# Strassen's seven products for four of eleven blocks of the up projection of a channel mixer

## The chip, the cores and the metric

One core of one Trainium2 chip runs the kernel. The metric is device time in microseconds (us) of one execution, lower is better; times are compared as medians over executions on the same chip. The engines of the core are named as the profile names them: PE is TensorE's matrix multiply, PEld its weight load, DVE is VectorE, ACT is ScalarE, POOL is GpSimd, SP is SyncE, which here only starts transfers.

## What is computed

The reference is a two-layer encoder on 512 tokens of 1024 channels. Each layer has a token mixer (layer 0: retention beside neighbourhood attention, layer 1: a Mamba-2 scan) and then the channel mixer that the change touches. Cut to that channel mixer:

```python
def conv_geglu_ffn(hn, w_up, conv_w, conv_b, w_down):
    u = depthwise_conv_centered(hn @ w_up, conv_w, conv_b)    # width 3 along the tokens
    gate, val = jnp.split(u, 2, axis=-1)                      # 2816 channels each
    return (jax.nn.gelu(gate, approximate=True) * val) @ w_down
...
    f = conv_geglu_ffn(rms_norm(x, norm_ffn_pre[layer]), ffn_w_up[layer], ...)
    x = x + rms_norm(f, norm_ffn_post[layer])
```

`w_up` is 1024 x 5632, `w_down` 2816 x 1024, all in float32. The change concerns the product `hn @ w_up`.

## The kernel before

**Precision.** A float32 product is made of three passes of TensorE in a 32-bit format of fewer mantissa bits (`R32`). Each operand is split into a high and a low part (`split`, L104: ScalarE casts the high part, L107; VectorE subtracts it from the original, L108), and `mm3` (L114) issues three matmuls into the same PSUM bank: high x high (L116), the stationary operand's low part x the other's high part (L117), and high x low (L118).

**Up projection.** `ffn` (L385) holds the normalised tokens feature-major, split already, in `E.xh` and `E.xl`: eight slices of 128 channels by 512 tokens. The 2816 gate and 2816 value channels are 22 tiles of 128 each. For a tile f, `wload` (L73) brings the gate weights, 128 x 1024 numbers, 512 KB, to a staging tile `wst`, `wunit` (L81) splits them to `whi` and `wlo`, and `proj_fm` (L127) runs 8 x 3 matmuls of 128 x 128 weights against 512 tokens into one PSUM bank; the value tile follows in the same way. I call such a load with its split and its 24 matmuls a unit. The first two tiles of a mixer are made in halves of 256 tokens, so that they can start before the last tokens are normalised. `tail` (L401) then makes the convolution out of PSUM (`conv`, L393: one step on ScalarE, L396, two on VectorE, L397 and L398), the GELU on ScalarE (L403) and the product gate x value on VectorE (L405) into `H`, 22 x 512 columns.

**Buffers.** There are 3 staging tiles, 4 each of `whi` and `wlo`, 2 of `gain` (a row of norm weights on all partitions), 7 of `tmp`, and eight PSUM banks, four in `mm` and four in `px` (L38 to L48). The up projection uses the four `mm` banks, two a tile.

**Down projection.** `down_strassen` (L278) already makes the down product by Strassen's method in Winograd's form. `sums` (L262) has the quarters of `w_down` added by accumulating transfers on GpSimd's queue (L274), into DRAM; these are cut into 32 `chores`, two of which are released after each tile, each waiting for the last matmul issued so far (`chore`, L68). The four quarters of `H` are combined by VectorE in `raw` (L308): the first difference (L311) goes into a tile `s3` of its own, the others into `H` in place. `prepare` (L322) splits them. The operand of the first of the seven products is split in `ffn`, L439 to L443, after tile 14 (`f == HK + 3`), into the buffers `b1h` and `b1l`. 

**Order.** The program is written in one stream. A scheduler places each instruction on its engine's queue by the order of the program and by when it reckons the operands and buffers ready; `high_priority(60)` moves a weight split ahead by 60 places. On the chip each queue then runs in that fixed order, with semaphores between the engines. All weight loads are on SyncE's queue.

Of the kernel before, what the change touches and what calls it, by code (L numbers as in the profile page):

```python
# [8 lines left out]
F32 = mybir.dt.float32  # L9
R32 = mybir.dt.float32r  # L10
# [3 lines left out]
ALU = mybir.AluOpType  # L14
# [3 lines left out]
P = 128  # L18
S = 512
NT = S // P  # L20
D = 1024
# [3 lines left out]
NF = FFN // P  # L25
HK = NF // 2
HW = S // 2
# [250 lines left out]
def down_strassen(E, big, pool, w, ts, H, s3, first, g_post, done):  # L278
# [7 lines left out]
    k0 = [0]  # L286

    def stage(i, u, cols):
        st = pool.tile([P, 1024], F32, name="wx") if k0[0] % 4 == 3 else E.wst.tile([P, 1024], F32, name="wst")
        k0[0] += 1  # L290
        nc.sync.dma_start(st[:, :cols], quarters(*i)[u])
        return st[:, :cols]
# [15 lines left out]
    def raw(i):  # L308
        tt, stt = nc.vector.tensor_tensor, nc.vector.scalar_tensor_tensor
        if i == 1:  # L310
            tt(s3, A11, A21, op=ALU.subtract)  # L311
            return s3
        if i == 2:
            tt(A21, A22, A21, op=ALU.subtract)
            stt(A11, A11, -1.0, A21, op0=ALU.mult, op1=ALU.subtract)
            return A11
        if i == 6:
            stt(A11, A12, -1.0, A11, op0=ALU.mult, op1=ALU.subtract)
            return A11
        return {3: A22, 4: A21, 5: A12}[i]  # L320
# [16 lines left out]
    for i, (src, bank) in enumerate(seq):  # L337
# [32 lines left out]
        op = nxt  # L370
        for t in range(2):
            if i in (0, 1, 2):
                kept[i, t] = pool.tile([P, 512], F32, name=f"k{i}{t}")
# [10 lines left out]

def ffn(E, w_up, cw, w_down, ts, g_post_row, done, w1=None):  # L385
# [3 lines left out]
    with ExitStack() as ctx:  # L389
# [3 lines left out]
        def conv(ps, s, f):  # L393
            w = lambda i: cwt[:, s, f, i:i + 1]
# [6 lines left out]
        def tail(f, pg, pv):  # L401
            g = conv(pg, 0, f)
            nc.scalar.activation(g, g, AF.Gelu_apprx_tanh)  # L403
            v = conv(pv, 1, f)
            nc.vector.tensor_tensor(H[:, f], g, v, op=ALU.mult)  # L405
# [11 lines left out]
        s3 = hp.tile([P, HK, HW], F32, name="s3")  # L417
        cwt = cp.tile([P, 2, NF, 4], F32, name="cwt")
        nc.sync.dma_start(cwt, cw)
        p0 = [[E.mm.tile([P, S], F32, name="mm") for s in range(2)] for f in range(2)]  # L420
# [6 lines left out]
        for f in range(2):  # L427
            tail(f, *p0[f])
        for f in range(2, NF):
            ps = []  # L430
# [8 lines left out]
            if f == HK + 3:  # L439
# [5 lines left out]
        down_strassen(E, hp, cp, w_down, ts, H, s3, first, g_post, done)  # L445
# [887 lines left out]
```

## Time and profile before

| what | value |
|---|---|
| timed runs, median of 3 | 1386.52 us (1384.4 to 1386.54) |
| profiled execution, its own time | 1384.75 us |
| its span | 1383.0 us |
| mean granted TensorE clock | 0.998 |
| HBM read, written | 221.01 MB, 51.64 MB |

The two channel mixers lie in the middle and at the end of the span: the one of layer 0 from about 272 to 640 us, the one of layer 1 from about 1031 to 1383 us. In each the up projection comes first, the down projection last; in layer 0 the down products start at 515.7 us, in layer 1 at 1270.9 us.

How to read what is shown of the profile: in a row of a group stand the line of the kernel, the engine, the operation, the output and inputs by the program's names, their shape and the count, then the busy time in us and the mean of one in ns, then the engine's idle time just before these instructions and what ended it. In the order of time, a line begins with the start and the length in us. In a table of windows, each engine has its busy time and, in brackets, its instructions; then come the granted clock, the busy share of the transfer engines and GB/s. Matmuls are pipelined: their records overlap, and the distance between starts tells how fast they go.

### The profile page before, as it was taken

How to read it: one execution, taken by the hardware profiler on the slowest of the kernel's cores; microseconds unless marked ns; L12 is line 12 of the kernel's file. 1: busy time of each engine (PE TensorE's matmuls, PEld its weight loads, DVE VectorE, ACT ScalarE, POOL GpSimd, SP SyncE). 2: the span in 40 equal slices, each digit the busy share in tenths (PEclk: the TensorE clock that was granted, in tenths of full speed). 3: DMA queues.
4: the chain of work that ended last, by engine and by line, in shares of the span. 5: the costliest groups of instructions: out<-in, count | busy, mean ns of one | idle time of the engine just before them, and what ended most of it. 6: DMA issues, size and time to landing. Idle time of an engine off the chain costs nothing.

```text
span 1383.0 us, 18079 instructions
## 1 busy us (share of the span) xinstructions
PE 1356.4 (98%) x6776; PEld 1119.3 (81%) x6776; DVE 985.0 (71%) x1402; ACT 758.2 (55%) x1233; POOL 113.6 (8%) x130
## 2 busy tenths in 40 slices
PE   7999999999999999999999999999999999999997
PEld 6877777898888888888778788787888888888886
DVE  7378888655565559697878785898786556556976
ACT  5357666443343346664878787487554434334563
POOL 0011110100011100020000110010010001110000
PEclk9999999999999999999999999999999999999999
DMA  8443222236679926553566464174445668983654
GB/s 295 145 141 105 90 87 95 69 143 230 233 204 233 236 88 187 197 202 127 144 180 191 125 186 158 54 208 119 138 133 172 217 228 223 226 220 96 200 177 144
DMA packets 69368, 229.81 MB, mean 166 GB/s; under 512 B 8352, under 2 KB 9120, under 8 KB 68768
## 3 DMA queue, kind: packets, MB, share of 16 engines
q1 hardware_dynamic: 54224, 167.30, 37.1%
q0 software_dynamic: 7168, 46.14, 13.6%
q10 hardware_dynamic: 7888, 15.21, 4.1%
q8 instruction: 54, 0.88, 0.3%
q14 instruction: 34, 0.28, 0.1%
HBM read 221.01 MB, written 51.64 MB: 197 GB/s over the span
## 4 chain that ended last, share of the span: by engine, by line
PE 85%; DVE 5%; ACT 4%; DMA 2%; issue 2%; POOL 1%; SPq 0%; DVEq 0%; POOLq 0%; ACTq 0%
PE mm L116 25%; PE mm L118 25%; PE mm L117 25%; DMA pb<-pd 2%; PE pi L999 1%; PE st L948 1%; PE py L1019 1%; ACT pb L978 1%; DVE wlo L108 1%; PE pt L173 1%; PE y L674 1%; DVE xs L164 1%; PE pt L892 1%; ACT whi L107 1%; DMA wst<-in_ab_v 0%
## 5 line engine op out<-in xcount | busy, mean ns | idle before, releaser
L116 PE MATMUL mm<-xh,whi 128*128 128x512 f32 (+1 forms) x1216 | 463.9, 382 | 1.0 <-ACT z L918 0.5
L118 PE MATMUL mm<-xl,whi 128*128 128x512 f32 (+2 forms) x1216 | 463.2, 381 | 1.0 <-DVE xl L108 0.5
L117 PE MATMUL mm<-xh,wlo 128*128 128x512 f32 (+2 forms) x1216 | 462.8, 381 | 1.0 <-DVE wlo L108 1.0
L108 DVE TENSOR_TENSOR wlo<-wst,whi 128x1024 fp32r<-128x1024 f32 (+1 forms) x232 | 281.0, 1215 | 72.7 <-ACT whi L107 72.1
L107 ACT CAST whi<-wst 128x1024 fp32r<-128x1024 f32 (+1 forms) x232 | 238.5, 1032 | 107.2 <-PE mm L117 63.5
L116 PEld LDWEIGHTS mm<-xh,whi 128*128 128x128 f32 x1216 | 228.3, 188 | 45.9 <-issue 2.5
L118 PEld LDWEIGHTS mm<-xl,whi 128*128 128x128 f32 (+1 forms) x1216 | 228.1, 188 | 45.5 <-issue 1.3
L117 PEld LDWEIGHTS mm<-xh,wlo 128*128 128x128 f32 (+1 forms) x1216 | 228.4, 188 | 44.2 <-DVE wlo L108 1.4
L397 DVE SCALAR_TENSOR_TENSOR cv<-mm,cwt,cv 128x511 f32<-128x511 f32 x88 | 65.9, 749 | 171.7 <-ACT cv L396 171.7
L396 ACT ACTIVATE cv<-mm,cwt 128x512 f32<-128x512 f32 x88 | 68.7, 780 | 200.4 <-PE mm L118 200.4
L978 ACT ACTIVATE pb<-pb,tok 128x128 f32<-128x128 f32 x256 | 80.9, 392 | 10.1 <-DMA pb<-pd 8.7
L398 DVE SCALAR_TENSOR_TENSOR cv<-mm,cwt,cv 128x511 f32<-128x511 f32 x88 | 66.0, 750 | 2.8
L116 PE MATMUL mm<-whi,ab1h 128*128 128x512 f32 x164 | 64.0, 390 | 0.0
L118 PE MATMUL mm<-wlo,ab1h 128*128 128x512 f32 x164 | 63.9, 390 | 0.0
L117 PE MATMUL mm<-whi,ab1l 128*128 128x512 f32 x164 | 63.8, 389 | 0.0
L403 ACT ACTIVATE cv<-cv 128x512 f32<-128x512 f32 x44 | 27.8, 633 | 44.5 <-DVE cv L398 44.4
L912 DVE SCALAR_TENSOR_TENSOR xf<-mm,cwt,xf 128x511 f32<-128x511 f32 (+1 forms) x64 | 47.6, 745 | 6.3 <-ACT xf L909 5.9
L274 POOL DMA_DIRECT2D ts<-in_f_down x48 | 30.0, 650 | 268.5 <-PE mm L118 266.0
L1031 POOL TENSOR_TENSOR sq<-sq 128x512 f32<-128x512 f32 x11 | 17.5, 1594 | 308.8 <-ACT sq L1025 245.1
L116 PE MATMUL mm<-whi,yh 128*128 128x512 f32 x104 | 40.8, 394 | 1.7 <-DVE xf L912 1.7
L117 PE MATMUL mm<-whi,yl 128*128 128x512 f32 x104 | 41.1, 395 | 0.0
L116 PE MATMUL mm<-whi,xh 128*128 128x512 f32 x104 | 40.7, 398 | 0.0
(308 smaller groups left out, 2121.6 us busy)
## 6 DMA issues: line engine op xcount, KB each, us to landing
wst<-in_f_up SPq DMA_DIRECT2D x88, 512.0 KB
ts<-in_f_down POOLq DMA_DIRECT2D x48, 704.0 KB, 5.8
wst<-in_c_fm SPq DMA_DIRECT2D x40, 512.0 KB
wst<-ts SPq DMA_DIRECT2D x32, 512.0 KB
pb<-pd ACTq DMA_DIRECT2D x29, 512.0 KB
wst<-in_f_down SPq DMA_DIRECT2D x24, 512.0 KB
ts<-ts POOLq DMA_DIRECT2D x16, 704.0 KB, 8.2
wst<-in_ab_fm SPq DMA_DIRECT2D x20, 512.0 KB
```

Of the source, the lines that this page charges most:

```text
L107: first = self.nc.scalar.copy(hi, src)
L108: second = self.nc.vector.tensor_tensor(lo, src, hi.bitcast(F32), op=ALU.subtract)
L116: mm(out, lh, rh, start=first, stop=False)
L117: mm(out, ll, rh, start=False, stop=False)
L118: self.product = mm(out, lh, rl, start=False, stop=last)
L274: out.append(lambda i=i, src=src, j=j, c=c, kw=kw: gp.dma_start(part(ts, i, c), part(src, j, c), **kw))
L396: nc.scalar.activation(o, ps, AF.Identity, scale=w(1), bias=w(3))
L397: nc.vector.scalar_tensor_tensor(o[:, 1:], ps[:, :S - 1], w(0), o[:, 1:], op0=ALU.mult, op1=ALU.add)
L398: nc.vector.scalar_tensor_tensor(o[:, :S - 1], ps[:, 1:], w(2), o[:, :S - 1], op0=ALU.mult, op1=ALU.add)
L403: nc.scalar.activation(g, g, AF.Gelu_apprx_tanh)
L912: nc.vector.scalar_tensor_tensor(r[:, a], ps[:, b], wc(j), r[:, a], op0=ALU.mult, op1=ALU.add)
L978: nc.scalar.activation(pb[:, dr, c], pb[:, dr, c], AF.Identity, scale=1.0 - 2 * dr, bias=tok[:, 0, c, dr * H + h:dr * H + h + 1])
```

## The change

In each mixer the tiles 6 and 7, 10 and 11, 14 and 15, and 18 and 19 become blocks of two gate and two value tiles. Such a block is one matrix product of 512 channels (256 gate, 256 value) by 1024 by 512 tokens; each side is halved, and `up_strassen` makes the quarters' product from seven products of 256 x 512 x 256 instead of eight. The other seven pairs of tiles stay as they were.

- *Token operands.* `combos` makes four sums and differences of the token quarters (`R1`, `S3`, `S2`, `S4`) on VectorE and splits them, one in each of tiles 2 to 5. It reads the quarters back as high + low into the part of `H` that tiles 14 to 21 will fill. The split results lie in the buffers `b1h`, `b1l`, `s3` and `e2` until the last block. Three operands are the split tokens themselves.
- *Weight operands.* Four loads of 512 KB bring the weight quarters, three to staging tiles and one to a `gain` tile. VectorE makes four sums of them in place; each of seven operands is split to `whi` and `wlo`, with the priority of the weight splits.
- *Products.* Each is 2 x 4 x 3 matmuls of 128 x 128 weights against 256 tokens. Product 1, 3, 5 and 7 go into the banks `a` (`mm`), 2 and 4 into `b`, 6 into `d` (both `px`); 3, 4, 5 and 7 add to what stands in their bank. After products 1, 2, 3, 5 and 7 ScalarE copies the two banks' state out to `G`, `V` or a temporary tile; after 4, 5 and 6 VectorE adds.
- *Tails.* The convolutions of a block read `G` and `V` in SBUF. `V` holds the negative, so that a table `cwn` with the sign turned is made once.
- *Moves.* The split of the first down operand comes after tile 20 instead of 14; the first difference of the down product takes the buffer `s3` that `S2` held; the kept results and a staging tile of the down projection share buffers with `G` and `V`. Chores: two after products 3 and 6 of a block.

The diff, without its blank lines:

```diff
--- before.py
+++ after.py
@@ -275,7 +275,7 @@
     return out
-def down_strassen(E, big, pool, w, ts, H, s3, first, g_post, done):
+def down_strassen(E, big, pool, w, ts, H, first, g_post, done):
@@ -286,7 +286,7 @@
     k0 = [0]
     def stage(i, u, cols):
-        st = pool.tile([P, 1024], F32, name="wx") if k0[0] % 4 == 3 else E.wst.tile([P, 1024], F32, name="wst")
+        st = pool.tile([P, 1024], F32, name="wx", tag="k3") if k0[0] % 4 == 3 else E.wst.tile([P, 1024], F32, name="wst")
         k0[0] += 1
         nc.sync.dma_start(st[:, :cols], quarters(*i)[u])
         return st[:, :cols]
@@ -308,6 +308,7 @@
     def raw(i):
         tt, stt = nc.vector.tensor_tensor, nc.vector.scalar_tensor_tensor
         if i == 1:
+            s3 = big.tile([P, HK, HW], F32, name="s3")
             tt(s3, A11, A21, op=ALU.subtract)
             return s3
         if i == 2:
@@ -368,9 +369,11 @@
             if uu == (1,):
                 nxt = prepare(i + 1)
         op = nxt
+        if i in (0, 1, 2):
+            m = pool.tile([P, 2, 512], F32, name="k", tag=f"k{i}")
+            kept.update({(i, t): m[:, t] for t in range(2)})
         for t in range(2):
             if i in (0, 1, 2):
-                kept[i, t] = pool.tile([P, 512], F32, name=f"k{i}{t}")
                 nc.scalar.copy(kept[i, t], bank[t])
             else:
                 j, tok, n = {3: (2, 0, 0), 4: (1, 0, 1), 5: (0, 2, 0)}[i]
@@ -382,6 +385,114 @@
     E.late += [lambda s=s: E.finish(s, st, done) for s in LATE]
+UP = (6, 10, 14, 18)
+def combos(E, pool, raw):
+    tt, stt = E.nc.vector.tensor_tensor, E.nc.vector.scalar_tensor_tensor
+    f32 = lambda ap: ap.bitcast(F32)
+    lower, upper = slice(0, HW), slice(HW, S)
+    out = {}
+    block = lambda k, c: (slice(None), slice(4 * k, 4 * k + 4), c)
+    def whole(i, k, c):
+        b = block(k, c)
+        tt(raw[:, i], f32(E.xh[b]), f32(E.xl[b]), op=ALU.add)
+        return raw[:, i]
+    def parts(n, tag, src):
+        x = pool.tile([P, 2, 4, HW], R32, name="x" + n, tag=tag)
+        E.split(x[:, 0], x[:, 1], src)
+        out[n] = x[:, 0], x[:, 1]
+    for n, k, c in (("A11", 0, upper), ("A12", 1, upper), ("A22", 1, lower)):
+        out[n] = E.xh[block(k, c)], E.xl[block(k, c)]
+    r1, a21 = whole(0, 1, lower), whole(1, 0, lower)
+    tt(r1, r1, a21, op=ALU.subtract)
+    parts("R1", "b1h", r1)
+    yield out
+    s2 = whole(2, 0, upper)
+    tt(a21, s2, a21, op=ALU.subtract)
+    parts("S3", "b1l", a21)
+    yield out
+    stt(s2, s2, -1.0, r1, op0=ALU.mult, op1=ALU.subtract)
+    parts("S2", "s3", s2)
+    yield out
+    s4 = whole(3, 1, upper)
+    stt(s4, s4, -1.0, s2, op0=ALU.mult, op1=ALU.subtract)
+    parts("S4", "e2", s4)
+    yield out
+def up_strassen(E, w_up, f, X, G, V):
+    nc, tc = E.nc, E.tc
+    low, high = slice(0, HW), slice(HW, S)
+    def load(pool, name, s, h):
+        st = pool.tile([P, 1024], F32, name=name)
+        nc.sync.dma_start(st.rearrange("p (f c) -> p f c", f=2),
+                          w_up[s, f:f + 2, :, h * 512:h * 512 + 512].rearrange("f p c -> p f c"))
+        return st
+    def parts(st):
+        hi, lo = E.whi.tile([P, 1024], R32, name="whi"), E.wlo.tile([P, 1024], R32, name="wlo")
+        E.split(hi, lo, st)
+        return hi, lo
+    add = lambda o, x, y: nc.vector.tensor_tensor(o, x, y, op=ALU.add)
+    q = {}
+    def weights(i):
+        with tc.high_priority(60):
+            if i == 0:
+                q[11] = load(E.wst, "wst", 0, 0)
+                return parts(q[11])
+            if i == 1:
+                q[12], q[22] = load(E.wst, "wst", 1, 0), load(E.wst, "wst", 1, 1)
+                add(q[11], q[11], q[12])
+                add(q[12], q[12], q[22])
+                return parts(q[12])
+            if i == 2:
+                q[0] = E.gain.tile([P, D], F32, name="gain")
+                add(q[0], q[11], q[22])
+                return parts(q[0])
+            if i == 3:
+                q[21] = load(E.gain, "gain", 0, 1)
+                add(q[0], q[0], q[21])
+                return parts(q[0])
+            return parts(q[{4: 11, 5: 21, 6: 22}[i]])
+    a = [E.mm.tile([P, S], F32, name="mm") for _ in range(2)]
+    b, d = ([E.px.tile([P, S], F32, name="pu", tag="px") for _ in range(2)] for _ in range(2))
+    order = ("A11", a), ("S3", b), ("S2", a), ("A22", b), ("R1", a), ("A12", d), ("S4", a)
+    for i, (n, bank) in enumerate(order):
+        hi, lo = weights(i)
+        more = i in (2, 3, 4, 6)
+        for j in range(2):
+            for k in range(4):
+                c = slice(j * 512 + k * P, j * 512 + k * P + P)
+                E.mm3(bank[j][:, :HW], hi[:, c], lo[:, c], X[n][0][:, k], X[n][1][:, k], not more and k == 0, k == 3, more)
+        if i == 4:
+            t = E.tmp.tile([P, 2, HW], F32, name="w5", tag="tmp")
+        for j in range(2):
+            r = bank[j][:, :HW]
+            if i in (3, 5):
+                o = G[:, j, low if i == 3 else high]
+                add(o, r, o)
+            else:
+                o = t[:, j] if i == 4 else {0: G[:, j, high], 1: V[:, j, low], 2: G[:, j, low], 6: V[:, j, high]}[i]
+                nc.scalar.copy(o, r)
+        if i == 4:
+            add(V[:, :, low], t, V[:, :, low])
+        if i in (2, 5):
+            E.chore(2)
 def ffn(E, w_up, cw, w_down, ts, g_post_row, done, w1=None):
@@ -390,18 +501,18 @@
         hp, cp = (ctx.enter_context(tc.tile_pool(name=n, bufs=1)) for n in ("ffn_h", "ffn_c"))
         H = hp.tile([P, NF, S], F32, name="H")
-        def conv(ps, s, f):
-            w = lambda i: cwt[:, s, f, i:i + 1]
+        def conv(ps, s, f, neg=False):
+            w = lambda i: (cwn[:, f] if neg and i < 3 else cwt[:, s, f])[:, i:i + 1]
             o = E.tmp.tile([P, S], F32, name=f"cv{s}", tag="tmp")
             nc.scalar.activation(o, ps, AF.Identity, scale=w(1), bias=w(3))
             nc.vector.scalar_tensor_tensor(o[:, 1:], ps[:, :S - 1], w(0), o[:, 1:], op0=ALU.mult, op1=ALU.add)
             nc.vector.scalar_tensor_tensor(o[:, :S - 1], ps[:, 1:], w(2), o[:, :S - 1], op0=ALU.mult, op1=ALU.add)
             return o
-        def tail(f, pg, pv):
+        def tail(f, pg, pv, neg=False):
             g = conv(pg, 0, f)
             nc.scalar.activation(g, g, AF.Gelu_apprx_tanh)
-            v = conv(pv, 1, f)
+            v = conv(pv, 1, f, neg)
             nc.vector.tensor_tensor(H[:, f], g, v, op=ALU.mult)
         def extra(tags):
@@ -414,9 +525,10 @@
         behind = E.turned[1][1] if w1 else None
         w0 = [[u0, u1], [E.wunit(w_up[0, 1], extra(("b1h", "b1l")), st, behind=behind),
                          E.wunit(w_up[1, 1], extra(("e2",)), behind=behind)]]
-        s3 = hp.tile([P, HK, HW], F32, name="s3")
         cwt = cp.tile([P, 2, NF, 4], F32, name="cwt")
         nc.sync.dma_start(cwt, cw)
+        cwn = cp.tile([P, NF, 3], F32, name="cwn")
+        nc.vector.tensor_scalar(cwn, cwt[:, 1, :, :3], -1.0, None, op0=ALU.mult)
         p0 = [[E.mm.tile([P, S], F32, name="mm") for s in range(2)] for f in range(2)]
         for c in range(2):
             for i in range(4):
@@ -426,7 +538,16 @@
                     E.flush()
         for f in range(2):
             tail(f, *p0[f])
+        make = combos(E, hp, H[:, 14:].rearrange("p (n g) s -> p n (g s)", n=4).rearrange("p n (k c) -> p n k c", k=4))
         for f in range(2, NF):
+            if f in UP or f - 1 in UP:
+                if f in UP:
+                    G, V = (cp.tile([P, 2, S], F32, name=n, tag=t) for n, t in
+                            ((("G", "k0"), ("V", "k1")) if UP.index(f) % 2 else (("G", "k2"), ("V", "k3"))))
+                    up_strassen(E, w_up, f, X, G, V)
+                    for j in range(2):
+                        tail(f + j, G[:, j], V[:, j], True)
+                continue
             ps = []
             for s in range(2):
                 behind = w1 and f == 2
@@ -436,13 +557,15 @@
                 E.proj_fm(ps[-1], w)
             tail(f, *ps)
             E.chore(2)
-            if f == HK + 3:
+            if f < UP[0]:
+                X = next(make)
+            if f == NF - 2:
                 first = [hp.tile([P, HK, HW], R32, name="a" + n, tag=n) for n in ("b1h", "b1l")]
                 for k in range(0, HK, 4):
                     c = slice(k, min(k + 4, HK))
                     E.split(first[0][:, c], first[1][:, c], H[:, c, HW:])
         g_post = E.bcast(g_post_row)
-        down_strassen(E, hp, cp, w_down, ts, H, s3, first, g_post, done)
+        down_strassen(E, hp, cp, w_down, ts, H, first, g_post, done)
 def log1p_exp_neg(E, alloc, z):
```

## The prediction

> **What bounds the kernel now.** I read the page first, then the chain of waits, then the windows of the two channel mixers (up projection and down projection), then the groups kept apart by shape, and last the order of time around one tile.
>
> ```profile
> span 1383.0 us, 18079 instructions
> PE 1356.4 (98%) x6776; PEld 1119.3 (81%) x6776; DVE 985.0 (71%) x1402; ACT 758.2 (55%) x1233; POOL 113.6 (8%) x130
> PE 85%; DVE 5%; ACT 4%; DMA 2%; issue 2%; POOL 1%; SPq 0%; DVEq 0%; POOLq 0%; ACTq 0%
> ```
>
> The reader is to see that TensorE (PE) holds 85% of the chain that ended last. The profiled execution took 1384.75 us, its span is 1383.0 us. A busy share of 98% says little by itself, because matmuls overlap; what counts is how far apart they start, so I took that from the order of time.
>
> ```profile
> 385.32 0.78 ACT L396 ACTIVATE cv<-mm,cwt 128x512 f32<-128x512 f32 x1 [2.37 <-PE mm L118]
> 390.76 0.78 ACT L396 ACTIVATE cv<-mm,cwt 128x512 f32<-128x512 f32 x1 [3.73 <-PE mm L118]
> 396.20 0.78 ACT L396 ACTIVATE cv<-mm,cwt 128x512 f32<-128x512 f32 x1 [2.36 <-PE mm L118]
> ...
> 294.81 0.28 PE L116 MATMUL mm<-xh,xb1h 128*128 128x256 f32 x1
> 294.93 0.28 PE L117 MATMUL mm<-xh,xb1l 128*128 128x256 f32 x1
> ...
> 297.93 0.28 PE L118 MATMUL mm<-xl,xe 128*128 128x256 f32 x1
> ```
>
> Each 128-channel tile of the up projection is a gate unit and a value unit of 24 matmuls of 512 columns, and ScalarE's first step on a finished unit comes every 5.44 us: 226.7 ns for one matmul. The kernel already has matmuls of 256 columns, in the first two tiles of each up projection: between 294.81 and 297.93 us lie 26 steps, 120.0 ns each. So half the columns take 53% of the time, not 50%. The next view is the busy time of each engine in stretches of that mixer.
>
> ```profile
> core 0: us, PE busy (x) PEld busy (x) DVE busy (x) ACT busy (x) POOL busy (x), PEclk, DMA share, GB/s
> 440.00:490.00 50.00, 50.00 (x222) 41.44 (x221) 27.21 (x33) 19.04 (x24) 7.00 (x8) 1.00 0.89 219
> 1280.00:1330.00 50.00, 50.00 (x222) 41.42 (x221) 40.92 (x31) 29.40 (x33) 0.00 (x0) 1.00 0.61 194
> 1042.00:1052.00 10.00, 10.00 (x86) 10.00 (x85) 7.06 (x8) 7.19 (x9) 0.00 (x0) 1.00 0.50 158
> ```
>
> In the up stage (440 to 490) PE runs without a gap at the full granted clock, VectorE (DVE) is busy 54% and ScalarE (ACT) 38%. In the down stage (1280 to 1330) VectorE is busy 82%, and PE still starts 222 matmuls in 50 us, as many as beside a VectorE at 54%: a VectorE at 82% does not by itself cost PE anything. In the stretch of 256 columns (1042 to 1052) the weight loads (PEld) are busy all 10.00 us. So PE is the bound in the stage that is changed, and a matmul saved there is time saved as long as the operands come in time.
>
> **The change part by part.** *Matmuls.* A block is two tiles: four units, 96 matmuls of 512 columns, 4 x 5.44 = 21.76 us. Strassen's form makes seven products, each of 2 output tiles x 4 contraction slices x 3 passes = 24 matmuls of 256 columns, 24 x 0.1200 = 2.88 us, and 7 x 2.88 = 20.16 us. That saves 1.60 us a block; four blocks in each of two mixers make 12.8 us. The ratio of multiplications alone, 7/8, would promise 2.72 us a block; the other 1.12 us go into the price of 72 more instructions.
>
> The Trainium skill, "TensorE: Matmul & The Clock Gate", section "Back-to-back issue gap", speaks against the change: in a stream of weight loads and matmuls it gives about 81 ns a matmul at 128 columns and 131 ns at 512, which on a straight line is an estimated 98 ns at 256, so a block would go from 96 x 131 = 12.6 us to 168 x 98 = 16.5 us and the whole kernel lose some 31 us. Here the trace does not agree, with 226.7 and 120.0 ns, and the sum goes by the rows.
>
> *Weights.* Before, a block splits four units of 1024 columns into a high and a low part; now it splits seven and makes four sums first.
>
> ```profile
> L108 DVE TENSOR_TENSOR wlo<-wst,whi 128x1024 fp32r<-128x1024 f32 x225 | 276.4, 1232 | 72.7 <-ACT whi L107 72.1
> L107 ACT CAST whi<-wst 128x1024 fp32r<-128x1024 f32 x225 | 234.1, 1045 | 105.8 <-PE mm L117 63.1 <-PE mm L118 21.4 <-PE pd L117 8.1
> L396 ACT ACTIVATE cv<-mm,cwt 128x512 f32<-128x512 f32 x88 | 68.7, 780 | 200.4 <-PE mm L118 200.4
> L398 DVE SCALAR_TENSOR_TENSOR cv<-mm,cwt,cv 128x511 f32<-128x511 f32 x88 | 66.0, 750 | 2.8
> L405 DVE TENSOR_TENSOR H<-cv,cv 128x512 f32<-128x512 f32 x44 | 30.2, 687 | 0.3
> L403 ACT ACTIVATE cv<-cv 128x512 f32<-128x512 f32 x44 | 27.8, 633 | 44.5 <-DVE cv L398 44.4
> L660 DVE TENSOR_TENSOR sd<-sc,toep 128x256 f32<-128x256 f32 x32 | 11.4, 415 | 0.0
> L881 ACT COPY tok<-pt 128x256 f32<-128x256 f32 x2 | 0.8, 375 | 0.6 <-PE pt L880 0.6
> ```
>
> VectorE in a block before: 4 splits x 1.232 + two tails of (4 x 0.750 + 0.687) = 4.93 + 7.37 = 12.3 us of 21.76. After: 7 splits 8.62, four sums at the same width 4.93, the same tails 7.37, four additions out of PSUM at 0.415 and one of 512 columns at 0.687, 2.35: 23.3 us. That is more than the block's own 20.16 us. But the tails of a block run beside the next two ordinary tiles, which ask 12.3 of 21.76: over the pair 35.6 of 41.9 us, 85%, near the down stage's 82%. What must be ready in the block for PE is the splits and sums alone, 13.6 us, and those stand ahead in the priority order. ScalarE: 7 x 1.045 + 10 copies x 0.375 + two tails of (2 x 0.780 + 0.633) = 15.5 us, with an ordinary pair's 8.6 together 24 of 41.9 us. Both engines fit, and I take nothing; the cover is PE's 41.9 us. If the tails did not move out of the block, VectorE's 23.3 us would set its length instead of 20.16, 3.1 us a block.
>
> *Buffers.* Four high and low weight buffers let a split run three units ahead. In the new block three units are 8.64 us instead of 16.3; a chain of a sum, a cast and a split is 1.23 + 1.05 + 1.23 = 3.5 us, so there remain 5 us for whatever is queued in front. The four quarter loads carry the bytes of the four unit loads. Three of them hold all three staging buffers, the longest until the seventh split; the load after it waits for that on SyncE's queue, and behind it all later loads. That the loads have room shows in what ended the idle time before uses of the staging tile:
>
> ```profile
>   PE mm L117: 63.5, 35
>   DMA wst<-in_f_up: 3.5, 2
> ```
>
> Casts waited for PE to free a buffer, and only twice, 3.5 us in all, for a transfer of these weights. I take nothing for the loads; their worst is those 3.5 us again.
>
> *Waits on PE's path that are new.* Two PSUM banks take several products one after the other, so products 3, 4, 5 and 7 must wait until ScalarE has copied out the earlier one, two copies of 0.375 us. Between lies one whole product, 2.88 us, so 2.1 us stay for a cast (1.05) that stands in front. I take zero, with the slow case as a rival below. The sums into the gate and value tiles are waited for by the tails alone, which have until a later tile needs the bank.
>
> *Token operands.* In tiles 2 to 5 of each mixer VectorE makes eight sums of 1024 columns and four splits, 12 x 1.23 = 14.8 us, and ScalarE four casts, in four tiles of 10.88 us whose idle share of VectorE is 46% or 20 us. Covered, but together with the first block's three weights ahead (three splits and three sums, 7.4 us) there is no idle time left. The small sign table adds one short VectorE step that waits at the start of the mixer for the load of its 88 KB.
>
> ```profile
> ts<-in_f_down POOLq DMA_DIRECT2D x48, 704.0 KB, 5.8
> ```
>
> Its price lies between 0 and the 5.8 us that a transfer of 704 KB takes from issue to landing; queued behind it on VectorE are the norms of the last token tiles and the splits of their transposes, for which PE waits. I take 0, since the load is an eighth as large and is issued ahead of the step.
>
> *The first down operand and its difference.* The split of the first down operand moves from tile 14 to tile 20, and the first difference, which took a slot at 400 us, must now wait for the buffer of the third product of the last block.
>
> ```profile
> L311 DVE TENSOR_TENSOR s<-H x2: 3092/3092/3092, 400.3 to 1155.6; 128x2816 f32<-128x2816 f32 x2
> 515.68 0.39 PE L116 MATMUL mm<-whi,ab1h 128*128 128x512 f32 x1
> 516.95 1.49 DVE L108 TENSOR_TENSOR axl<-s,axh 128x1280 fp32r<-128x1280 f32 x1 [2.76 <-ACT axh L107]
> 523.15 1.75 DVE L108 TENSOR_TENSOR axl<-s,axh 128x1536 fp32r<-128x1536 f32 x1
> 538.59 1.75 DVE L108 TENSOR_TENSOR ab1l<-H,ab1h 128x1536 fp32r<-128x1536 f32 x1
> ```
>
> The down products start at 515.68, and each takes 66 matmuls, 15.0 us; the second needs its operand at 530.6 and has it at 524.9, the third at 545.6 and has it at 540.3. The room is 5.7 and 5.3 us. New in front of that: 3.1 us (the difference), 2816 columns of splitting at about 1.2 us per 1024, 3.4 us, and one tail more, 3.7 us: 10.2 us against VectorE's idle 10 us in the last two ordinary tiles. So it is nearly covered, and the price is 0 to 10.2 - 5.3 = 4.9 us a mixer.
>
> *Sum.* Unknown small stalls: in the present trace the largest wait of a main matmul on a late weight is one row,
>
> ```profile
> PE mm L117 <- DVE wlo L108: 1.0, 1, 1.0
> ```
>
> that is, 1.0 us where VectorE was crowded at a mixer's start. I take 1.0 us for each of the two mixers, nearer to the uncrossed 0 of the 82% window than to 4.9. So 1384.75 - 12.8 + 2.0 = 1373.95 us against the profiled execution. The three timed runs lie at 1384.4, 1386.52 and 1386.54, so the median is 1.8 us above the profiled one; on the median's level the same sum gives 1375.7. I forecast 1375.0, between the two.
>
> **The rivals.** *Shortfall.* The first block with the token operands and the last one lose their 3.1 us each, and the start of the down products its 4.9: 11.1 us a mixer would give 1384.75 - 12.8 + 22.2 = 1394.2; half of it gives 1383.1, which I take as the time of this case. For it: 85% is above any window of the present trace. Against it: no matmul of either mixer waits today beyond that 1.0 us.
>
> *The copies out of PSUM come late (slower).* One mechanism: ScalarE's queue is in order, and a cast waiting for VectorE's sum stands in front of the copies that free a bank. Chain after a product: split in progress 1.23, sum 1.23, cast 1.05, two copies 0.75, 4.26 us against 2.88: PE stops 1.38 us, four times a block, eight blocks: 44 us, 1384.75 - 12.8 + 44 = 1416. It decides from 0.4 us for each of the 32 reuses on. The row of ScalarE's L403, 44.4 us idle behind VectorE, shows that such in-order waiting exists; against it stands that the weights are to be made three units ahead and ScalarE is below 60%. The Trainium skill, same page, opening table (engine queue depth), calls the queues of ScalarE and VectorE strict first in, first out, with which that row agrees.
>
> *Spacing.* Break-even for a matmul of 256 columns is 21.76 us / 168 = 129.5 ns. If here weight loads stopped overlapping and each took the whole length of its record,
>
> ```profile
> L116 PEld LDWEIGHTS mm<-xh,whi 128*128 128x128 f32 x1208 | 227.3, 188 | 45.2 <-issue 2.5 <-ACT z L918 0.7 <-ACT xh L107 0.7
> ```
>
> a block would take 168 x 0.188 = 31.6 us, and the kernel 79 us more, 1463. This is the shape that the skill's rule above has in view. The 26 steps of 120.0 ns with the same three passes speak against it.
>
> *It does not do what it says*, or the 256-column matmuls run at half of 226.7: 8 x 2.72 = 21.8 us gained, 1363. Nothing in the rows is for it.
>
> **How the numbers follow.** Forecast 0.76, shortfall 0.11, late copies 0.09, spacing 0.02, half time 0.02. About 0.2%, 2.8 us, is what a measurement of this kernel can tell. Faster by more than that means below 1383.7: the forecast, half time and a small part of the shortfall, 0.80. Within: the rest of the shortfall, 0.09. Slower: late copies and spacing, 0.11. The range begins at 1371.0 (all 12.8 us gained on the level of the fastest run, 1371.6, rounded down) and ends at 1385.0, past the shortfall's 1383.1; outside lie late copies, spacing, half time and the tail of the shortfall, under 0.2.
>
> **What would show it right or wrong.** Right: 256-column matmuls of the Strassen blocks 0.12 us apart, a block of 20.2 us between ordinary units of 5.44 us, VectorE about 85% busy over tiles 6 to 21 with PE at 50.00 in each window of 50 us, casts still ended by PE freeing a buffer. Wrong in the shortfall's way: idle time of PE or its loads behind VectorE's low part in the first and last block, or at the start of the down products. Wrong in the copies' way: gaps of PE behind ScalarE's copies inside a block, and a longer block in all eight. If the span fell by 12.8 us with no such gap, the 2.0 us of stalls were too much.

## The result and the profile after

The changed kernel took 1371.95 us (median of six runs, 1370.24 to 1375.13) against 1385.94 us for the kernel before (six runs, 1384.4 to 1389.3). The ratio is 0.9899 with a 95% interval of 0.9884 to 0.9915: faster by 14.0 us, 1.0%. The forecast was 1375.0 us in a range of 1371.0 to 1385.0; the median lies 3.05 us below the forecast and 0.95 us above the lower end of the range. The profiled execution took 1372.97 us, its span is 1371.2 us, 11.8 us below the span before.

From the page of the changed kernel, the span, the engines' busy times and the chain that ended last by engine:

```profile
span 1371.2 us, 19491 instructions
PE 1344.3 (98%) x7352; PEld 1136.2 (83%) x7352; DVE 1088.5 (79%) x1524; ACT 815.2 (59%) x1345; POOL 111.5 (8%) x130
PE 83%; ACT 6%; DVE 5%; DMA 3%; issue 2%; POOL 1%; DVEq 0%; SPq 0%; POOLq 0%; ACTq 0%
```

There are 576 more matmuls, 72 for each of eight blocks, and VectorE (DVE) has 103 us more to do; PE's share of the chain is about what it was. Where the time went shows in three places in the order of time of PE: the start of tile 2, the first matmuls of the first block, and the start of the down products.

```profile
299.15 0.40 PE L116 MATMUL mm<-xh,whi 128*128 128x512 f32 x1
...
342.70 0.28 PE L116 MATMUL mm<-xh,whi 128*128 128x256 f32 x1
342.81 0.28 PE L117 MATMUL mm<-xh,wlo 128*128 128x256 f32 x1
342.93 0.28 PE L118 MATMUL mm<-xl,whi 128*128 128x256 f32 x1
...
510.46 0.39 PE L116 MATMUL mm<-whi,ab1h 128*128 128x512 f32 x1
```

I call the stretch from tile 2 to the first down product the up stage. It lasted 515.68 - 298.05 = 217.63 us before, and 510.46 - 299.15 = 211.31 us now; in the second mixer it went from 1270.91 - 1053.28 = 217.63 to 1259.43 - 1048.12 = 211.31 us. Twice 6.32 us make 12.64 us; all the rest of the span is 0.84 us longer. Ahead of the first up stage 1.10 us are added, where only the small sign table is new; the other runs below, which make the same table, reach tile 2 anywhere from 297.88 to 300.21 us, so no cause is shown for this part. Of the 14.0 us between the medians, 12.64 us are thus found in the up stages; no run gives the other 1.4 us a cause, and they are less than the spread of the executions (1370.24 to 1375.13). The windows of the first mixer after the change:

```profile
core 0: us, PE busy (x) PEld busy (x) DVE busy (x) ACT busy (x) POOL busy (x), PEclk, DMA share, GB/s
340.00:380.00 40.00, 40.00 (x257) 36.59 (x256) 31.64 (x38) 21.40 (x32) 3.87 (x8) 1.00 0.65 237
460.00:500.00 40.00, 40.00 (x257) 36.59 (x256) 37.28 (x44) 23.85 (x35) 2.28 (x3) 1.00 0.79 212
500.00:550.00 50.00, 50.00 (x222) 41.40 (x221) 43.08 (x36) 29.89 (x33) 0.00 (x0) 1.00 0.51 161
```

VectorE is busy 79% around the first block, 93% around the last and 86% at the start of the down products, and PE has no gap in any of them. In the whole of both up stages no wait of PE is on record.

### The profile page after: what moved, and what is told of

The parts are those of the page before. It is cut to its first block, busy times and chain, and to the rows that moved or that the text cites. A ratio compares the mean times of both kernels' runs of the same rounds, so it can differ in the third digit from the quotient of the medians.

```text
span 1371.2 us, 19491 instructions
## 1 busy us (share of the span) xinstructions
PE 1344.3 (98%) x7352; PEld 1136.2 (83%) x7352; DVE 1088.5 (79%) x1524; ACT 815.2 (59%) x1345; POOL 111.5 (8%) x130
## 4 chain that ended last, share of the span: by engine, by line
PE 83%; ACT 6%; DVE 5%; DMA 3%; issue 2%; POOL 1%; DVEq 0%; SPq 0%; POOLq 0%; ACTq 0%
PE mm L116 23%; PE mm L118 23%; PE mm L117 23%; PE pu L118 2%; PE pu L117 2%; PE pu L116 2%; PE pi L1122 1%; PE st L1071 1%; ACT pb L1101 1%; DMA pb<-pd 1%; PE py L1142 1%; ACT whi L107 1%; DVE wlo L108 1%; DMA wst<-in_c_fm 1%; PE pt L173 1%
## 5 line engine op out<-in xcount | busy, mean ns | idle before, releaser
L116 PE MATMUL mm<-xh,whi 128*128 128x512 f32 (+1 forms) x1024 | 382.5, 374 | 0.8 <-ACT z L1041 0.4
L118 PE MATMUL mm<-xl,whi 128*128 128x512 f32 (+1 forms) x1024 | 381.6, 373 | 1.0 <-DVE xl L108 0.5
L117 PE MATMUL mm<-xh,wlo 128*128 128x512 f32 (+1 forms) x1024 | 381.3, 373 | 1.0 <-DVE wlo L108 1.0
L116 PEld LDWEIGHTS mm<-xh,whi 128*128 128x128 f32 x1024 | 192.6, 188 | 35.9 <-issue 2.3
L118 PEld LDWEIGHTS mm<-xl,whi 128*128 128x128 f32 x1024 | 192.2, 188 | 35.6 <-issue 1.3
L117 PEld LDWEIGHTS mm<-xh,wlo 128*128 128x128 f32 x1024 | 192.6, 188 | 34.2 <-DVE wlo L108 1.4
L507 ACT ACTIVATE cv<-mm,cwt 128x512 f32<-128x512 f32 x56 | 43.5, 777 | 68.8 <-PE mm L118 68.7
L508 DVE SCALAR_TENSOR_TENSOR cv<-mm,cwt,cv 128x511 f32<-128x511 f32 x56 | 41.7, 745 | 22.2 <-ACT cv L507 22.2
L509 DVE SCALAR_TENSOR_TENSOR cv<-mm,cwt,cv 128x511 f32<-128x511 f32 x56 | 41.8, 746 | 0.9
```

The lines of the kernel that those rows point to most:

```text
L116: mm(out, lh, rh, start=first, stop=False)
L117: mm(out, ll, rh, start=False, stop=False)
L118: self.product = mm(out, lh, rl, start=False, stop=last)
L507: nc.scalar.activation(o, ps, AF.Identity, scale=w(1), bias=w(3))
L508: nc.vector.scalar_tensor_tensor(o[:, 1:], ps[:, :S - 1], w(0), o[:, 1:], op0=ALU.mult, op1=ALU.add)
L509: nc.vector.scalar_tensor_tensor(o[:, :S - 1], ps[:, 1:], w(2), o[:, :S - 1], op0=ALU.mult, op1=ALU.add)
```

## The experiments

All times are from five rounds beside the kernel before on the same chip; not all runs are on one chip, so that the ratios, and not the times, are to be compared between runs. "Up stages" are those of the profiled execution, first and second mixer. The changed kernel stands at 211.31 and 211.31 us.

### The moves alone

Edit: no blocks, no token operands; the later split, the shared buffers and the sign table stay.

```diff
-UP = (6, 10, 14, 18)
+UP = ()
...
-            if f < UP[0]:
-                X = next(make)
```

> No block is made by the seven products: all tiles are ordinary, but the later split of the first down operand, the shared buffers and the sign table stay. Theory (the whole gain is fewer columns on TensorE, everything else lies beside it): the time of the kernel before, within 0.2%, and the down products start 217.6 us after tile 2 begins, as before. Rival (the moves themselves gain or cost): more than 3 us to either side, with a gap of TensorE at the start of the down products.

Measured: 1385.33 us, ratio 0.9992 (0.9982 to 1.0001), span 1383.0 us; up stages 217.63 and 217.62 us. The moves are free, and the gain comes with the blocks. The token operands are not in this run, but in the next.

### Two blocks

```diff
-UP = (6, 10, 14, 18)
+UP = (6, 14)
```

> Two blocks in each mixer, tiles 6, 7 and 14, 15. Theory: 1.58 us a block, 4 blocks, 6.3 us faster than before, half of the whole change; the up stage 214.5 us. Rival (a fixed part, from the token operands or the moves): the first two blocks bring less than half, the up stage over 215.5 us.

Measured: 1378.06 us, ratio 0.9936 (0.9922 to 0.9949); up stages 214.47 and 214.46 us. That is 3.16 us for two blocks, 1.58 a block, exactly half of the 6.32 us for four. In the up stages there is no fixed part. The medians tell this less sharply: two blocks are 9.0 us faster than the kernel before on that chip (1387.07 us), where half of 14.0 would be 7.0, at the edge of the interval.

### The price of narrower matmuls by itself

Edit to the run of the moves alone: the eight tiles are ordinary but in halves of 256 tokens.

```diff
+HALVED = (6, 7, 10, 11, 14, 15, 18, 19)
...
-                E.proj_fm(ps[-1], w)
+                for c in (0, HW) if f in HALVED else ():
+                    E.proj_fm(ps[-1], w, c, c + HW)
+                if f not in HALVED:
+                    E.proj_fm(ps[-1], w)
```

> No block by seven products; the same eight tiles of each mixer are made by the ordinary method but with each unit as two halves of 256 tokens, 48 matmuls instead of 24. Theory: the price of an instruction beyond its columns is 2 x 120.0 - 226.7 = 13.3 ns, so 24 x 13.3 ns = 0.32 us a unit, 32 units, 10.2 us slower than before; up stage 222.7 us. Rival (the price lies in the change of banks and operands in a block, not in the narrower matmul): no more than 2 us slower.

Measured: 1397.87 us, ratio 1.0078 (1.0063 to 1.0094). The ends of the up stage in the order of time of PE:

```profile
298.14 0.40 PE L116 MATMUL mm<-xh,whi 128*128 128x512 f32 x1
...
520.97 0.39 PE L116 MATMUL mm<-whi,ab1h 128*128 128x512 f32 x1
```

Both up stages took 222.83 us, 5.20 us longer than before for 16 units, 13.5 ns for each of 384 additional matmuls a mixer. The price of an instruction beyond its columns is shown by itself, and the rival falls.

### Copies out of PSUM made twice

```diff
                 nc.scalar.copy(o, r)
+                nc.scalar.copy(o, r)
```

> The changed kernel with every copy out of PSUM in a block made twice, ten more ScalarE instructions of 0.37 us a block. Theory (a bank's copies have a whole product of 2.88 us to be made in): the up stage stays at 211.3 us within 0.5 us. Rival (the copies stand on TensorE's path): at least 0.75 us at each of four reuses in eight blocks, 24 us slower than the changed kernel, TensorE idle behind the copies.

Measured: 1373.73 us, ratio to before 0.9911 (0.9896 to 0.9926); up stages 211.30 and 211.31 us. The copies' own length does not count: a product between two uses of a bank covers twice as many. A cast that stands in front of the copies is another matter, which this run does not test.

### Seven blocks side by side

```diff
-UP = (6, 10, 14, 18)
+UP = (6, 8, 10, 12, 14, 16, 18)
```

> Seven blocks in each mixer without ordinary tiles between them, tiles 6 to 19. If TensorE alone set the pace: 14 x 1.58 = 22.1 us faster than before, up stage 206.6 us. Theory: in a block VectorE's instructions sum to 23.3 us, some 21 us busy when their overlaps are taken off, against 20.16 us of TensorE; with no ordinary tiles to catch up in, VectorE falls behind by about 1 us a block and up to 7 us a mixer, so the gain is 8 to 20 us, with idle time of TensorE's weight loads behind VectorE's low parts or at the start of the down products. Rival (VectorE never binds): the full 22.1 us.

Measured: 1429.57 us, ratio 1.0311 (1.0290 to 1.0331); up stages 242.09 and 239.44 us. The loss is far beyond what I expected of VectorE. Windows of the first mixer, then VectorE's waits for loads in the first mixer, then the waits of PE's loads in the whole run:

```profile
360.00:380.00 20.00, 16.73 (x122) 16.18 (x122) 17.33 (x21) 12.11 (x20) 1.93 (x4) 0.88 0.59 212
400.00:420.00 20.00, 16.08 (x126) 15.47 (x127) 13.60 (x17) 9.20 (x15) 3.22 (x4) 0.99 0.97 221
```

```profile
DVE wst L447 <- DMA wst<-in_f_up: 23.3, 6, 6.4
```

```profile
PEld pu L117 <- DVE wlo L108: 20.7, 20, 2.0
PEld pu L116 <- ACT whi L107: 20.5, 19, 2.8
```

PE waits for split weights, but VectorE is busy only 87% and 68% of these windows: it stood itself, six times, for 23.3 us, ahead of a weight sum whose quarter had not landed. So the limit that came first was the loads and not VectorE's work. PE pays twice, as its order of time shows:

```profile
375.36 0.80 PE L116 MATMUL pu<-xh,whi 128*128 128x256 f32 x2 [2.55 <-ACT whi L107]
376.88 0.58 PE L117 MATMUL pu<-xh,wlo 128*128 128x256 f32 x1 [0.72 <-DVE wlo L108]
...
380.24 0.41 PE L118 MATMUL pu<-xl,whi 128*128 128x256 f32 x1
380.45 0.41 PE L116 MATMUL pu<-xh,whi 128*128 128x256 f32 x1
380.67 0.41 PE L117 MATMUL pu<-xh,wlo 128*128 128x256 f32 x1
```

```profile
372.00:376.00 4.00, 1.45 (x9) 1.11 (x8) 3.90 (x6) 2.55 (x4) 0.97 (x2) 0.92 0.50 180
376.00:380.00 4.00, 3.28 (x15) 3.13 (x15) 4.00 (x4) 2.69 (x5) 0.00 (x0) 0.50 0.59 220
380.00:384.00 4.00, 4.00 (x28) 4.00 (x27) 1.93 (x4) 1.42 (x2) 0.00 (x0) 0.73 0.78 266
```

After the stops the same matmuls start 0.21 us apart instead of 0.12. In windows of half a microsecond the granted clock is 1.00 up to 375.0 us, 0.50 from 375.5 to 382.0 and 1.00 again from 382.5: it falls at about the end of the stop of 2.55 us, at 375.36, and ahead of the stop of 0.72 us. Over the window of 360 to 380 us that makes 0.88.

### Seven blocks with the fourth quarter out of the staging buffers

Edit to the run of seven: the quarter that is held until the seventh split is loaded into columns of `H` that no tile has filled yet.

```diff
-                q[12], q[22] = load(E.wst, "wst", 1, 0), load(E.wst, "wst", 1, 1)
+                q[12], q[22] = load(E.wst, "wst", 1, 0), load(None, "", 1, 1)
...
+                    i = UP.index(f)
+                    c = 16 if i == 0 else 18 if i % 2 else 20
+                    up_strassen(E, H[:, c:c + 2].rearrange("p k s -> p (k s)"), w_up, f, X, G, V)
```

> Seven blocks side by side, as in the run of seven blocks whose up stages took 242 and 239 us, but the fourth weight quarter is loaded into columns of the result tile that are still free, two places in turn, and not into a staging buffer. Theory (there the loads of the next block came late, since the quarter holds its buffer until the seventh split): the waits for these loads go, and the up stage falls to between 206.6 (TensorE alone) and 216 us (VectorE 1 us a block behind). Rival (VectorE's own work is the limit of seven blocks): still over 230 us, with VectorE busy near 100%.

Measured: 1380.75 us, ratio 0.9956 (0.994 to 0.9972); up stages 214.05 and 214.80 us.

```profile
380.00:420.00 40.00, 38.95 (x314) 37.77 (x313) 39.72 (x49) 27.82 (x45) 6.26 (x8) 1.00 0.87 211
420.00:460.00 40.00, 38.95 (x314) 37.78 (x313) 39.66 (x49) 27.08 (x44) 6.06 (x7) 1.00 1.01 236
```

One buffer was worth 28 and 25 us of the two up stages. Now VectorE is busy 99%, with PE at 97%, and no cast waits for a load in either up stage: this is VectorE's limit, and it costs 7.5 and 8.2 us a mixer over the 206.6 us of TensorE alone.

### Five and six blocks

Five blocks as they are, five with the fourth quarter in `H`, and six with it there.

```diff
-UP = (6, 10, 14, 18)
+UP = (6, 9, 12, 15, 18)
...
+UP = (6, 8, 11, 13, 16, 18)
```

> Five blocks in each mixer (6, 9, 12, 15, 18) with one ordinary tile between two blocks; nothing else differs from the changed kernel. If only TensorE sets the pace: up stage 217.63 - 5 x 1.58 = 209.7 us, 15.8 us faster than before, 3.2 us faster than the changed kernel. Theory (what limits the number of blocks is the staging buffer that the fourth quarter holds until the seventh split, so that the next block's load comes late): a block and a single ordinary tile last 31.0 us, and the load has room, so 209.7 to 212 us. Rival (VectorE's work in a block, 23.3 us, limits): VectorE is asked for 29.4 of 31.0 us, 95%, and the up stage is 212 us or more with idle time behind VectorE's low parts.

Measured: 1389.28 us, ratio 1.0016 (1.0006 to 1.0026); up stages 218.93 and 219.26 us. My theory had the limit right, as the next run shows, but not its reach: with a single ordinary tile between blocks the load has no room either.

> Five blocks in each mixer as in the earlier run of five (up stages 218.9 and 219.3 us), with the fourth weight quarter in free columns of the result tile. Theory (the staging buffer was the limit of five blocks): no wait for these loads, up stage 209.7 to 211 us, 2 to 3 us faster than the changed kernel in the whole. Rival (VectorE at 95% of a block and a single ordinary tile was the limit): still over 215 us.

Measured: 1375.86 us (1372.65 to 1379.3), ratio 0.9921 (0.9907 to 0.9936); up stages 211.79 and 210.52 us. The casts' waits for a load, first of five blocks as they are, then with the quarter in `H`:

```profile
ACT whi L107 <- DMA wst<-in_f_up: 34.8, 14, 4.8
```

```profile
ACT whi L107 <- DMA wst<-in_f_up: 6.3, 2, 3.2
```

The buffer was the limit of five blocks. But of the 1.6 us a mixer that a fifth block should bring, only -0.5 and 0.8 us came, and the whole is not faster than four blocks: the intervals overlap, and the median is not the lower one.

> Six blocks in each mixer (6, 8, 11, 13, 16, 18), the fourth quarter in free columns of the result tile. TensorE alone: 208.2 us. VectorE: two blocks and one ordinary tile ask 2 x 23.3 + 6.2 = 52.8 us by durations, some 48 us busy, against 51.2 us. Theory: VectorE is near its end but still covered, 208.2 to 211 us; the best of all if it is covered. Rival (VectorE's limit already bites here as with seven): 212 us or more.

Measured: 1380.33 us, ratio 0.9960 (0.9945 to 0.9975); up stages 214.97 and 212.47 us instead of 208.2. Above four blocks the fifth brings nothing that these runs can tell, and the sixth and seventh cost more than they bring.

### More VectorE work, and the order of one load

Edit: four sums more in a block, written to an unused tile.

```diff
+            if i in (1, 2, 3):
+                for _ in range(2 if i == 1 else 1):
+                    add(E.junk[:, :1024], q[11], q[11])
```

> The changed kernel with four more VectorE sums of 1024 columns a block, results unused, placed ahead of the weight sums; VectorE is asked for 28.2 us a block and 40.5 of 41.9 us over a block and two ordinary tiles, 97% by the sum of durations and some 90% busy. Theory (VectorE is covered while its mean over block and ordinary tiles stays below TensorE's time): up stage 211.3 to 213 us. Rival (what is asked inside a block counts): VectorE's excess of 28.2 - 20.2 = 8 us a block is lost at least in part, the up stage longer than 220 us.

Measured: 1390.57 us (1382.75 to 1397.87), ratio 1.0031 (1.0009 to 1.0053); up stages 212.65 and 224.72 us. The twelve executions differ by up to 15 us, and the profile shows one of them. Its first up stage agrees with the theory. The second lies, by its length, where the rival has it, but is not lost block by block: PE's waits there sum to 9.3 us, and one of them is 6.34. The chain behind it, in the order of time of SyncE, VectorE, ScalarE and PE:

```profile
1225.33 0.34 SPq L76 DMA_DIRECT2D wst<-in_f_up  x1
1225.72 0.43 SPq L438 DMA_DIRECT2D gain<-in_f_up  x1
```

```profile
1224.08 1.22 DVE L108 TENSOR_TENSOR wlo<-wst,whi 128x1024 fp32r<-128x1024 f32 x1
...
1229.94 0.74 DVE L511 SCALAR_TENSOR_TENSOR cv<-mm,cwt,cv 128x511 f32<-128x511 f32 x1
1235.85 1.23 DVE L447 TENSOR_TENSOR gain<-gain 128x1024 f32<-128x1024 f32 x1 [5.17 <-DMA gain<-in_f_up]
```

```profile
1229.27 0.63 ACT L492 COPY G<-mm 128x256 f32<-128x256 f32 x2
1237.11 1.04 ACT L107 CAST whi<-gain 128x1024 fp32r<-128x1024 f32 x1 [7.20 <-DVE gain L447]
1238.06 1.04 ACT L107 CAST whi<-wst 128x1024 fp32r<-128x1024 f32 x1
1239.01 0.64 ACT L492 COPY V<-pu 128x256 f32<-128x256 f32 x2
```

```profile
1239.42 0.58 PE L116 MATMUL pu<-xh,whi 128*128 128x256 f32 x1 [6.34 <-ACT V L492]
```

The quarter for the last of the block's four sums (the expectations below call it the third) was asked for behind the next tile's load, at 1225.72, and used at 1235.85. VectorE stood for it 5.17 us, ScalarE's cast stood for VectorE 7.20 us, and the copies that free a bank stood behind the cast: PE stopped 6.34 us. This is the mechanism of the prediction's slower rival, set off by a late load. It was late by its place on SyncE's queue: the next tile's load in front of it waited for a staging buffer until the split at 1224.08 had ended, and the quarter's followed it within 0.1 us. In the changed kernel, in the same block, the quarter's load stands in front and the tile's load behind it:

```profile
1203.51 0.43 SPq L438 DMA_DIRECT2D gain<-in_f_up  x1
1214.20 0.34 SPq L76 DMA_DIRECT2D wst<-in_f_up  x1
```

So the added sums also changed the order in which the scheduler placed the loads.

In the next two runs that load is asked for at the start of its block, with the added sums and then with five blocks:

```diff
                 q[11] = load(E.wst, "wst", 0, 0)
+                q[21] = load(E.gain, "gain", 0, 1)
...
-                q[21] = load(E.gain, "gain", 0, 1)
```

> The run with four more VectorE sums a block, whose second up stage took 224.7 us with one stop of TensorE of 6.3 us, but the load of the quarter that the third sum needs is asked for first in its block, not after the next tile's load on SyncE's queue. Theory (there a late load stood at the head of VectorE's queue, ScalarE's cast waited for the sum and the copies out of PSUM behind the cast): the stop goes, both up stages 211.3 to 214 us, though VectorE has as much to do. Rival (the added VectorE work itself cost it): one up stage at least still over 218 us.

Measured: 1380.25 us, ratio 0.9962 (0.9947 to 0.9977); up stages 215.19 and 215.24 us. The largest row of PE's waits for these copies in the whole run:

```profile
PE pu L116 <- ACT V L492: 3.7, 4, 1.1
```

The long stop went and 224.7 us became 215.2 with the same work on VectorE, so the work by itself was not what made that stop. But the first stage rose by 2.5 us, and both lie above my 214: 3.9 us a mixer over the changed kernel are left. PE's waits make 2.7 us of them in each up stage, all behind copies that stood behind a cast, and that cast stood for a sum of VectorE that waited for no load. These runs do not tell whether VectorE's added work or the new order of the loads makes them.

> Five blocks with the fourth quarter in free columns of the result tile (up stages 211.8 and 210.5 us) and the same earlier load of the quarter for the third sum. Theory (what was left there were late loads at the head of VectorE's queue): up stages 209.7 to 210.5 us, 1.5 to 3 us faster than the changed kernel, the best version. Rival (VectorE at 95% of block and single tile is what is left): no better than 211 us.

Measured: 1387.05 us, ratio 1.0001 (0.9989 to 1.0012); up stages 216.91 and 220.11 us, 5 and 10 us worse than without the earlier load. The theory fell. The order of time of VectorE, SyncE and ScalarE in the second mixer shows what the earlier load did:

```profile
1203.76 1.23 DVE L108 TENSOR_TENSOR wlo<-gain,whi 128x1024 fp32r<-128x1024 f32 x1 [1.12 <-ACT whi L107]
1204.90 1.22 DVE L108 TENSOR_TENSOR wlo<-wst,whi 128x1024 fp32r<-128x1024 f32 x1
```

```profile
1205.01 0.38 SPq L438 DMA_DIRECT2D gain<-in_f_up  x1
1206.14 4.65 SPq L438 DMA_DIRECT2D wst<-in_f_up  x2
```

```profile
1218.22 1.05 ACT L107 CAST whi<-wst 128x1024 fp32r<-128x1024 f32 x1 [5.93 <-DMA wst<-in_f_up]
```

There are two `gain` buffers, and this load goes out when the block before has split out of one (1203.76 us). The load of the first quarter, at 1206.14, now stands behind it. It would not have gone out sooner, since its own staging buffer came free only with the split of 1204.90. But it lands later: its cast stands 5.93 us for it and starts 12.1 us after the request. In the run without the earlier load the first quarter goes out first, and its cast starts 9.9 us after the request:

```profile
1194.38 5.15 SPq L438 DMA_DIRECT2D wst<-in_f_up  x2
```

```profile
1204.24 1.05 ACT L107 CAST whi<-wst 128x1024 fp32r<-128x1024 f32 x1 [3.21 <-DMA wst<-in_f_up]
```

One block earlier it is 11.6 us against 8.5. So the quarter that is needed last was brought ahead of the one that is needed first. That this alone makes the 5 and 10 us is not shown.

## Why the prediction was right, step by step

- **Matmuls.** Right. The forecast was 20.16 us a block; (211.31 - 12 x 10.88) / 4 = 20.19 us were measured. Two blocks brought half of what four did, and the matmuls in halves cost 13.5 ns each where 13.3 was worked out. One detail of the working is off: of the 1.12 us between 2.72 and 1.60, 72 more instructions at 13.3 ns make 0.96; the other 0.16 us are the eighth of the 96 old instructions' own price that 7/8 of the time also takes off. The rule of the Trainium skill ("TensorE: Matmul & The Clock Gate", section "Back-to-back issue gap") by which a matmul's distance falls too little with its width does not hold here: 0.12 us against 0.227.
- **VectorE and ScalarE covered.** Right for four blocks: VectorE was busy 81% from 340 to 500 us, where 85% was worked out, up to 93% in one window, and PE had no gap. Seven blocks with the loads mended show where the cover ends, at 99%.
- **Buffers and loads.** The step that was sized wrongly. I gave 3.5 us of waits for transfers as the worst and took nothing for them; the changed kernel has nine such waits of casts, and they sum to 19.4 us:

```profile
ACT whi L107 <- DMA wst<-in_f_up: 19.4, 9, 4.2
```

They cost PE nothing: no wait of PE is on record in the up stages, and splits were laid out to run three units ahead. But the runs of five and seven blocks show that this, and not VectorE, is the margin that is used up first. The sentence on the quarter that holds its buffer until the seventh split named the place; I gave it no price, and with seven blocks it was 25 to 28 us a mixer.
- **Waits on PE's path.** Zero was right for the changed kernel; doubled copies cost nothing. The rival's chain exists: with a late load at its head it stopped PE for 6.34 us, and without one, in the run with added sums and the earlier load, for 0.8 to 1.1 us at three places in the first mixer. The Trainium skill ("TensorE: Matmul & The Clock Gate", opening table) calls the queues of ScalarE and VectorE strict first in, first out; the copies that stood behind a cast while it stood for 7.20 us agree with that.
- **Token operands, moves, start of the down products.** Zero was right for the moves (217.63 us without blocks), and the down products start without a gap at a VectorE of 86%. The 4.9 us that I kept as an end of the range did not come.
- **Sum.** I forecast 12.8 us gained in the up stages and 2.0 us lost to small stalls. The up stages gained 12.64 us, and the 2.0 us were too much. Their size was taken from a row that does not belong to the stage: the wait of 1.0 us is not at the start of a channel mixer but in the token mixer of layer 1, at 714.70 us before and 708.81 us after, and it is in the profile of both kernels.

```profile
PE mm L117 <- DVE wlo L108: 1.0, 1, 1.0
714.70 0.50 PE L117 MATMUL mm<-xh,wlo 128*128 128x512 f32 x1 [0.97 <-DVE wlo L108]
```

On the profiled execution the sum said 1373.95 us and 1372.97 were measured: 2.0 us too many for stalls, against 0.16 us less gained and 0.84 us more in the rest of the span. The other 2 us between forecast and median come from where the profiled executions lie, below the median before and above it after; that the median stayed inside the range by 0.95 us is in this part luck.

- **Late copies, spacing, half time, shortfall.** None came with four blocks. With five the gain was lost (ratio 1.0016), but by late loads and not by VectorE's work, which is what the shortfall was about.

## What to carry to other kernels

Strassen's method on a bound TensorE gains the columns saved less a fixed price for each matmul added, and both can be read from matmuls of the two widths that are already in a trace: here 13 ns of each matmul eat 41% of what 7/8 promises. Beside it, count for how long each staging buffer is held, not only how busy the engines are: a quarter that is needed first in a sum and again in the last product turns a short load into the next block's late one. Look at what stands at the head of each queue: a request that waits for a buffer held up one behind it that waited for none, and PE stopped 6.34 us. And before asking for a load earlier, look at which loads it then goes ahead of, since those land later.

## What the hardware showed that I had not expected

Short stops of PE cost more than their length. In the run of seven blocks, from about the end of a stop of 2.55 us (375.36 us) on, the granted clock was 0.50 until 382 us, and in the last 5 us of that the same 256-column matmuls started 0.213 us apart, 1.8 times the 0.120 us; in the windows of the changed kernel, without stops, the clock is 1.00. The Trainium skill, "TensorE: Matmul & The Clock Gate", section "Part 1: The HAM clock gate (the "warmup" mystery)", has the clock at half after an idle window of some 3.4 us; here shorter stops were enough: the one of 2.55 us, and in the second mixer of the same run a single one of 1.75 us that ended at 1252.57 us, with none over 0.3 us in the 6 us before it, after which the clock from 1254 to 1256 us is 0.51.
